# Opening of a hybrid gated-attention trunk: squares and scales of the second half's rows spread over the modulation's steps, products in three parts, one minimum pinned

## The chip, the cores and the metric

One NeuronCore of a Trainium2 chip runs the whole kernel. The metric is the device time of one execution in microseconds; the kernel before has a median of 1246.13 us over three runs (1244.64 to 1246.9).

## What is computed

One layer of a decoder trunk over 1024 rows of width 1024, all in float32. A conditioning vector gives shift and scale; the rows are normalised and modulated; one large projection of them feeds two gated linear attentions and their gates; both branches are merged and projected out. What matters here is the beginning:

```python
c_act = jax.nn.silu(c)
mod = c_act @ ada_w[l] + ada_b[l]
shift, scale, gate = jnp.split(mod, 3, axis=-1)
h = rms_norm(x, norm_w[l]) * (1.0 + scale[:, None, :]) + shift[:, None, :]
proj = h @ w_in[l]
...
log_a = jax.nn.log_sigmoid((ga @ alpha_w + alpha_b).astype(jnp.float32)) / GLA_GATE_TAU
```

The first columns of `proj` that are made are query and key of the second attention (GLA); the last line gives the decay of its four heads.

## The kernel before

**Arithmetic.** Each float32 operand of a large product is split into two parts of a faster type, `hi` by ScalarE's cast (L195) and `lo` by VectorE's subtraction (L196), and a product is the three matmuls hi*hi, hi*lo, lo*hi (`n` = 0, 1, 2 in `product`, L343).

**The opening** (L357 to L423) is written in the order in which TensorE, ScalarE and VectorE shall run it: those three are under a manual schedule from L158 to `order.close()` at L423. Behind that a scheduler orders the instructions. Each engine runs its own queue in order. The rows of `x` come in two halves of 512, each in four tiles of 128 rows. A half is normalised by `norm_x`: ScalarE squares a tile and sums (L204), takes a root (L206), VectorE inverts it (L207) and scales the tile in place (L208). `transpose_x` turns column block `d` of the four tiles on TensorE (L215) into one PSUM tile, which ScalarE copies out (L217). `make_h` applies the modulation on ScalarE (L224) and splits (L195, L196).

**The modulation** of the eight column blocks comes in five steps, `blocks` = (0), (1, 2), (3, 4), (5, 6), (7). For each step `load_mod` brings the weights, `add_mod` sums the upper half of the rows on VectorE (L256, L258), `mm_mod` does the lower half on TensorE (L268), `end_mod` adds both on VectorE (L274), sums over partitions on TensorE (L278) and leaves `modv` and `amul` (L281, L283), which `make_h` needs. While one step's column blocks go into the products, the next step is made: the loop at L368 interleaves `products(d, ns)`, which are six matmuls for each `n` (six groups of 128 columns: four for q, two for k, in the PSUM tiles `pd_177`, `pd_178` and `sc_ps`), with the steps of the next block. Step `bi == 3` also normalises the second half of the rows (L387).

**Behind the loop** stand two transposes and two `make_h` of the second half, the products of block 7, `make_ga` for the first half (L332, copied out by L334), and the six accumulators' copies `qk_out` on VectorE (L322, L324). `first_group` then does the products of the second half, and the generator `alpha_side` computes the decays of the four heads in pieces woven between them: two small products (L904), a bias (L906), a minimum on VectorE (L908) and a sum (L909), exponential (L914), logarithm (L917), a difference (L918) and an exponential (L921). Each `yield` says how many units of TensorE's work pass before the next piece.

**Loads** all go through SyncE's queue in the order written: weights of steps 0 and 1, three blocks of `w_in` between them, then step 2 and so on; the second half of `x` is asked for after step `bi == 1`. PSUM tiles `pm` come from a pool of two (`mtile`), so a third waits until the first has been read; the tiles `pd` also are two.

## Time and profile before

| what | value |
|---|---|
| median of 3 runs | 1246.13 us (1244.64 to 1246.9) |
| the profiled execution: its time, its span | 1243.66 us, 1242.0 us |
| TensorE busy | 1202.8 us (97%) |
| VectorE, ScalarE, GpSimd busy | 759.9, 535.3, 115.7 us |
| mean granted TensorE clock | 0.993 |
| moved by DMA | 168.82 MB |

The time of the profiled execution is 1.66 us over its span, which runs from the first instruction to the last. In the profile PE is TensorE, DVE VectorE, ACT ScalarE, POOL GpSimd and SP SyncE. A row of the instructions in order of time has start, duration (both us), engine, line, operation, the tile written and those read, and in brackets how long the engine was idle before it and whose end released it. A stage's row has for each engine the busy time and the count of instructions, then the granted TensorE clock, the share of time that the DMA engines were busy, and GB/s.

### The profile page before, as it was taken

The page shows a single profiled execution, that of the slowest core. Times are in us where ns is not written, and L with a number is a line of the kernel's source. Part 1 is how long each engine was busy: PE and PEld are TensorE (multiplying, and loading weights), DVE is VectorE, ACT ScalarE, POOL GpSimd, SP SyncE. Part 2 cuts the span into 40 slices and gives each one's busy share as a digit, 9 for nine tenths or more (in the row PEclk, how much of TensorE's full clock was granted, in tenths as well). Part 3 has the DMA queues.
Part 4 walks back from the last instruction along what each step waited for, and adds up shares of the span by engine and source line. Part 5 has one row for each costly group of instructions (what it writes and reads, how often), then busy time and mean ns, then how long its engine had stood idle before and what let it go on. Part 6 is the DMA issues. An engine that isn't in the chain of part 4 may idle for free.

```text
span 1242.0 us, 20840 instructions
## 1 busy us (share of the span) xinstructions
PE 1202.8 (97%) x8627; PEld 996.6 (80%) x8627; DVE 759.9 (61%) x1225; ACT 535.3 (43%) x786; POOL 115.7 (9%) x201
## 2 busy tenths in 40 slices
PE   5999999999999999999999999999999999998997
PEld 3676889889798888788887878877888887787786
DVE  5635535584848466877774366785422758979443
ACT  5547643434434234334323324457643644454222
POOL 4100000202111121011110101011100000000000
PEclk9989999999999999999999999999999999999999
DMA  9714010744544267265251112244547456235202
GB/s 325 258 52 136 24 28 19 260 157 145 170 151 147 81 200 244 96 187 166 74 186 52 51 35 69 75 156 169 184 158 243 154 186 195 77 102 178 110 35 101
DMA packets 126928, 168.82 MB, mean 136 GB/s; under 512 B 7019, under 2 KB 97185, under 8 KB 126834
## 3 DMA queue, kind: packets, MB, share of 16 engines
q1 hardware_dynamic: 115234, 129.53, 33.4%
q0 software_dynamic: 11552, 37.97, 8.0%
q8 instruction: 67, 1.10, 0.4%
q14 instruction: 27, 0.22, 0.1%
q10 hardware_dynamic: 48, 0.01, 0.0%
HBM read 125.53 MB, written 41.94 MB: 135 GB/s over the span
## 4 chain that ended last, share of the span: by engine, by line
PE 59%; issue 23%; DVE 8%; DMA 4%; ACT 3%; POOL 2%; SPq 0%; POOLq 0%; DVEq 0%; ACTq 0%
PE pd L518 14%; PE pd L1377 9%; PE sc_ps L1377 5%; PE pm L1377 4%; PE pd L343 3%; PE pd L620 2%; PE pd L621 2%; PE pd L622 2%; PE sc_ps L343 1%; DVE b L196 1%; PE pm L825 1%; PE pd L1147 1%; PE pd L1148 1%; PE pd L1149 1%; DMA b<-yh 1%
## 5 line engine op out<-in xcount | busy, mean ns | idle before, releaser
L518 PE MATMUL pd<-b,b 128*128 128x512 f32 x1632 | 386.7, 393 | 0.0
L518 PEld LDWEIGHTS pd<-b,b 128*128 128x128 f32 x1632 | 302.4, 188 | 64.3 <-issue 0.7
L1377 PE MATMUL pd<-b,b 128*128 128x512 f32 x720 | 175.5, 395 | 3.0 <-DVE b L930 1.5
L1377 PEld LDWEIGHTS pd<-b,b 128*128 128x128 f32 x720 | 134.4, 189 | 35.7 <-DVE b L930 1.9
L196 DVE TENSOR_TENSOR b<-b,b 128x1024 fp32r<-128x1024 f32 (+2 forms) x99 | 102.5, 1045 | 92.0 <-ACT b L195 75.3
L195 ACT CAST b<-b 128x1024 fp32r<-128x1024 f32 (+2 forms) x99 | 86.7, 888 | 109.1 <-PE pd L518 16.9
L1320 DVE TENSOR_TENSOR b<-b,b 128x1024 fp32r<-128x1024 f32 x56 | 68.2, 1222 | 68.8 <-ACT b L1319 50.5
L1319 ACT CAST b<-b 128x1024 fp32r<-128x1024 f32 x56 | 58.4, 1050 | 65.3 <-PE pd L1377 19.1
L1377 PE MATMUL sc_ps<-b,b 128*128 128x512 f32 x324 | 79.0, 391 | 0.9 <-ACT scT L770 0.9
L1377 PE MATMUL pm<-b,b 128*128 128x512 f32 x300 | 72.7, 390 | 3.3 <-DVE b L1320 3.3
L577 PE MATMUL pd<-b,b 128*128 128x256 f32 x256 | 74.6, 291 | 0.0
L579 PE MATMUL pd<-b,b 128*128 128x256 f32 x256 | 72.5, 283 | 0.0
L578 PE MATMUL pd<-b,b 128*128 128x256 f32 x256 | 72.4, 283 | 0.0
L1377 PEld LDWEIGHTS sc_ps<-b,b 128*128 128x128 f32 x324 | 60.4, 188 | 14.2 <-ACT scT L770 1.4
L1377 PEld LDWEIGHTS pm<-b,b 128*128 128x128 f32 x300 | 56.6, 189 | 15.6 <-DVE b L1320 3.7
L343 PE MATMUL pd<-b,b 128*128 128x512 f32 x192 | 56.6, 431 | 4.8 <-DVE b L322 2.6
L1298 DVE TENSOR_TENSOR b<-b,b 128x1024 fp32r<-128x1024 f32 x36 | 45.1, 1262 | 18.1 <-ACT b L1297 10.3
L1235 POOL DMA_DIRECT2D ws<-b x64 | 34.6, 541 | 192.6 <-DVE b L1229 87.3
L620 PE MATMUL pd<-b,b 128*128 128x512 f32 x128 | 51.3, 401 | 0.0
L343 PEld LDWEIGHTS pd<-b,b 128*128 128x128 f32 x192 | 37.3, 203 | 17.2 <-issue 3.4
L712 ACT COPY xb<-b 128x512 f32<-128x512 f32 x48 | 29.4, 620 | 48.8 <-PE sc_ps L692 26.6
L621 PE MATMUL pd<-b,b 128*128 128x512 f32 x128 | 50.0, 390 | 0.0
(269 smaller groups left out, 2010.6 us busy)
## 6 DMA issues: line engine op xcount, KB each, us to landing
b<-in_w_in_dram SPq DMA_DIRECT2D x66, 512.0 KB, 4.1
ws<-b POOLq DMA_DIRECT2D x64, 256.0 KB, 3.4
b<-ws SPq DMA_DIRECT2D x32, 512.0 KB, 4.4
b<-in_x_dram SPq DMA_DIRECT2D x16, 512.0 KB, 5.6
b<-in_ada_w_dram SPq DMA_DIRECT2D x32, 256.0 KB, 6.5
b<-in_w_branch_dram SPq DMA_DIRECT2D x16, 512.0 KB, 4.4
b<-h SPq DMA_DIRECT2D x14, 512.0 KB, 4.0
b<-in_w_in_dram SPq DMA_DIRECT2D x24, 256.0 KB, 3.8
```

The source lines that it names most:

```text
L195: nc.scalar.copy(hi, src)
L196: nc.vector.tensor_sub(lo, src, hi.bitcast(F32))
L343: nc.tensor.matmul(accs[f], wg(a, d, f), b[d][:, half * 512:half * 512 + 512], start=(d == 0 and n == 0), stop=(d == KT - 1 and n == 2))
L518: nc.tensor.matmul(ps[0:w, th * 512:(th + 1) * 512], a[:, k, 0:w], b[:, th * 512:(th + 1) * 512], start=(k == 0 and n == 0), stop=(k == KT ...
L577: nc.tensor.matmul(o, lh, hi[:, k % 4, :], start=(k == 0), stop=False)
L578: nc.tensor.matmul(o, lh, lo[:, k % 4, :], start=False, stop=False)
L579: nc.tensor.matmul(o, ll, hi[:, k % 4, :], start=False, stop=(k == KT - 1))
L620: nc.tensor.matmul(o, lh, hi[:, k % 2, :], start=(k == 0), stop=False)
L621: nc.tensor.matmul(o, lh, lo[:, k % 2, :], start=False, stop=False)
L1319: nc.scalar.copy(hi, t)
L1320: nc.vector.tensor_sub(lo, t, hi.bitcast(F32))
L1377: nc.tensor.matmul(o, a[:, sl], c, start=(p in (1, 5) and kt == 0 and n == 0), stop=(kt == 3 and n == 2), skip_group_check=True)
```

## The change

`norm_x` is cut into `square_x` (ScalarE's square and root) and `scale_x` (VectorE's inverse and scale), `transpose_x` into `turn_x` (TensorE) and `copy_x` (ScalarE); the computation is the same. In the opening the order changes: in the first step's loop `mm_mod(1)` and `end_mod(1)` stand between the three parts of the products, and block 3 is turned behind them, to be copied out within the next `make_h` loop. In step `bi == 3` two tiles of the second half are squared and scaled ahead of the products, the other two are squared behind the transposes and scaled behind `end_mod(4)`. Behind the loop, block 7's first products come ahead of the transposes, `make_h(1, 0)` behind all its products, and `make_h(1, 1)` behind the third `qk_out`. In `alpha_side` the minimum is kept in program order, and the pauses change.

```diff
--- before.py
+++ after.py
@@ -196,27 +196,35 @@
         nc.vector.tensor_sub(lo, src, hi.bitcast(F32))
         return hi, lo
 
-    def norm_x(half, xs):
-        for i, xt in enumerate(xs):
-            t = half * 4 + i
-            acc, r = ssx[:, t:t + 1], rsx[:, t:t + 1]
-            junk = S.get([D])
-            nc.scalar.activation(junk, xt, AF.Square, accum_out=acc)
-            S.free(junk)
-            nc.scalar.activation(r, acc, AF.Sqrt, bias=eps_t, scale=1.0 / D)
-            nc.vector.reciprocal(r, r)
-            nc.vector.tensor_scalar_mul(xt, xt, r)
-
-    def transpose_x(half, xs, d):
+    def square_x(t, xt):
+        acc, r = ssx[:, t:t + 1], rsx[:, t:t + 1]
+        junk = S.get([D])
+        nc.scalar.activation(junk, xt, AF.Square, accum_out=acc)
+        S.free(junk)
+        nc.scalar.activation(r, acc, AF.Sqrt, bias=eps_t, scale=1.0 / D)
+
+    def scale_x(t, xt):
+        r = rsx[:, t:t + 1]
+        nc.vector.reciprocal(r, r)
+        nc.vector.tensor_scalar_mul(xt, xt, r)
+
+    turned = {}
+
+    def turn_x(half, xs, d):
         if d % 2 == 0:
             hT[half, d // 2] = S.get([2, 512])
-        pt = mtile()
+        turned[half, d] = mtile()
         for i in range(4):
-            nc.tensor.transpose(pt[:, i * P:(i + 1) * P], xs[i][:, d * P:(d + 1) * P], ident)
-        dst = hT[half, d // 2][:, d % 2, :]
-        nc.scalar.copy(dst, pt)
+            nc.tensor.transpose(turned[half, d][:, i * P:(i + 1) * P], xs[i][:, d * P:(d + 1) * P], ident)
         if d == KT - 1:
             S.free(*xs)
+
+    def copy_x(half, d):
+        nc.scalar.copy(hT[half, d // 2][:, d % 2, :], turned.pop((half, d)))
+
+    def transpose_x(half, xs, d):
+        turn_x(half, xs, d)
+        copy_x(half, d)
 
     def make_h(half, d):
         b = hT[half, d // 2][:, d % 2, :]
@@ -356,7 +364,9 @@
     load_wg(3)
     load_wg(4)
     load_mod(2)
-    norm_x(0, x_t)
+    for i in range(4):
+        square_x(i, x_t[i])
+        scale_x(i, x_t[i])
     vec_rows(rows_a, 24, R_SH)
     transpose_x(0, x_t, 0)
     add_mod(0)
@@ -370,6 +380,8 @@
         nxt = range(blocks[bi + 1][0], sum(blocks[bi + 1])) if more else ()
         for d in ds:
             make_h(0, d)
+            if (0, d + 2) in turned:
+                copy_x(0, d + 2)
         if not more:
             break
         for d in nxt:
@@ -378,21 +390,30 @@
         if nd == 1:
             for d in nxt:
                 transpose_x(0, x_t, d)
+            products(d0, (0,))
+            mm_mod(bi + 1)
+            products(d0, (1,))
+            end_mod(bi + 1)
+            products(d0, (2,))
+            turn_x(0, x_t, nxt[-1] + 1)
+        else:
+            late = x_t2 if bi == 3 else ()
+            for i, xt in enumerate(late[:2]):
+                square_x(4 + i, xt)
+                scale_x(4 + i, xt)
             products(d0, (0, 1))
-            mm_mod(bi + 1)
-            products(d0, (2,))
-            end_mod(bi + 1)
-        else:
-            products(d0, (0, 1))
-            transpose_x(0, x_t, nxt[0])
-            if bi == 3:
-                norm_x(1, x_t2)
+            if bi > 1:
+                transpose_x(0, x_t, nxt[0])
+            for i, xt in enumerate(late[2:]):
+                square_x(6 + i, xt)
             mm_mod(bi + 1)
             products(d0, (2,))
             for d in nxt[1:]:
                 transpose_x(0, x_t, d)
             products(d0 + 1, (0,))
             end_mod(bi + 1)
+            for i, xt in enumerate(late[2:]):
+                scale_x(6 + i, xt)
             products(d0 + 1, (1, 2))
         if bi == 0:
             load_wg(5)
@@ -402,14 +423,13 @@
             load_mod(4)
         elif bi == 1:
             x_t2.extend(load_x(t) for t in range(4, 8))
+    products(KT - 1, (0,))
     for d in range(2):
         transpose_x(1, x_t2, d)
-    for d in range(2):
-        make_h(1, d)
-    products(KT - 1, (0,))
     for f in range(NG):
         for n in (1, 2):
             product(0, KT - 1, f, n)
+    make_h(1, 0)
     ga4, aw4 = S.get([T]), S.get([512])
     nc.gpsimd.memset(aw4, 0.0)
     for j in range(4):
@@ -420,6 +440,8 @@
     for f in range(NG):
         g_state[("q", f) if f < 4 else ("k", f - 4)] = qk_t[f]
         qk_out(f, 0, accs[f])
+        if f == 2:
+            make_h(1, 1)
     order.close()
 
     def first_group():
@@ -905,11 +927,11 @@
                                      start=True, stop=True)
                     nc.scalar.activation(zb[:, th * 512:(th + 1) * 512], pz, AF.Identity,
                                          bias=vec[:, R_AB + h:R_AB + h + 1])
-                nc.vector.tensor_scalar_min(m, zb, 0.0)
+                tc.keep_in_program_order(nc.vector.tensor_scalar_min(m, zb, 0.0))
                 nc.vector.scalar_tensor_tensor(zb, m, 2.0, zb, ALU.mult, ALU.subtract)
                 zs[h] = zb
                 alphas[h] = m
-                yield 4
+                yield 9 if h == 0 else 2
             for zb in zs.values():
                 nc.scalar.activation(zb, zb, AF.Exp)
             yield 4
@@ -920,7 +942,7 @@
             for h, zb in zs.items():
                 nc.scalar.activation(alphas[h], alphas[h], AF.Exp, scale=1.0 / TAU)
                 S.free(zb)
-            yield 6
+            yield 4
         S.free(ga4, aw4)
 
     def silu_done(store, key):
```

What this makes of the queues can't all be read from the diff. The rows below are the instructions of one engine in the order of its queue: line, operation, tile written and tiles read with their numbers, and shape. Lines of the change are those of its own file, about 8 higher at first and 22 higher later.

On **VectorE**, the end of step `bi == 3`: the sums of `add_mod(4)`, the second half's scales, the sum of `end_mod(4)` (`scT<-scT,pm`) and its `modv` and `amul`. Before:

```order
L258 SCALAR_TENSOR_TENSOR scT<-b_339,cs,scT 128x256 x3
L207 RECIPROCAL rsx<-rsx 128x1
L208 TENSOR_SCALAR b_425<-b_425,rsx 128x1024
L207 RECIPROCAL rsx<-rsx 128x1
L208 TENSOR_SCALAR b_427<-b_427,rsx 128x1024
L207 RECIPROCAL rsx<-rsx 128x1
L208 TENSOR_SCALAR b_429<-b_429,rsx 128x1024
L207 RECIPROCAL rsx<-rsx 128x1
L208 TENSOR_SCALAR b_431<-b_431,rsx 128x1024
L274 TENSOR_TENSOR scT<-scT,pm_565 128x256
L281 TENSOR_TENSOR modv<-pm_583,vec 128x2
L283 SCALAR_TENSOR_TENSOR amul<-modv,vec 128x1
```

In the change:

```order
L266 SCALAR_TENSOR_TENSOR scT<-b_344,cs,scT 128x256 x3
L208 RECIPROCAL rsx<-rsx 128x1
L209 TENSOR_SCALAR b_425<-b_425,rsx 128x1024
L208 RECIPROCAL rsx<-rsx 128x1
L209 TENSOR_SCALAR b_427<-b_427,rsx 128x1024
L282 TENSOR_TENSOR scT<-scT,pm_561 128x256
L289 TENSOR_TENSOR modv<-pm_579,vec 128x2
L291 SCALAR_TENSOR_TENSOR amul<-modv,vec 128x1
L208 RECIPROCAL rsx<-rsx 128x1
L209 TENSOR_SCALAR b_429<-b_429,rsx 128x1024
L208 RECIPROCAL rsx<-rsx 128x1
L209 TENSOR_SCALAR b_431<-b_431,rsx 128x1024
```

Two of the four pairs of reciprocal and scale now stand behind the step's end.

On **ScalarE**, the second half's first blocks: copies of the turned blocks (`b<-pm`), the modulation (ACTIVATE with `modv`), the casts, and the copy of `make_ga` (`b_640<-pm_651` before, `b_637<-pm_648` in the change). Before:

```order
L217 COPY b_603<-pm_604 128x512
L217 COPY b_603<-pm_610 128x512
L224 ACTIVATE b_603<-b_603,modv,amul 128x512
L195 CAST b_143<-b_603 128x512
L224 ACTIVATE b_603<-b_603,modv,amul 128x512
L195 CAST b_144<-b_603 128x512
L217 COPY b_779<-pm_780 128x512
L195 CAST b_822<-b_777 128x1024
L334 COPY b_640<-pm_651 128x512
L224 ACTIVATE b_779<-b_779,modv,amul 128x512
L195 CAST b_145<-b_779 128x512
```

In the change:

```order
L223 COPY b_609<-pm_610 128x512
L223 COPY b_609<-pm_616 128x512
L232 ACTIVATE b_609<-b_609,modv,amul 128x512
L195 CAST b_143<-b_609 128x512
L223 COPY b_779<-pm_780 128x512
L195 CAST b_822<-b_777 128x1024
L342 COPY b_637<-pm_648 128x512
L232 ACTIVATE b_609<-b_609,modv,amul 128x512
L232 ACTIVATE b_779<-b_779,modv,amul 128x512
L195 CAST b_144<-b_609 128x512
L195 CAST b_145<-b_779 128x512
```

The modulation of block 1 of the second half and its cast (`b_144`) stood ahead of the copy of `make_ga` and stand behind it, and block 2's modulation comes in between.

On **VectorE** again, the end of `first_group` and the first heads of `alpha_side`: `b_966` and `b_965` belong to head 0, `b_1000` and `b_999` (before), `b_1041` and `b_1040` (in the change) to head 1; `pd_177`, `pd_178` and `sc_ps` are the accumulators that `qk_out` empties; the rows that write `xb` begin the attention of head 0. Before:

```order
L908 TENSOR_SCALAR b_966<-b_965 128x1024
L909 SCALAR_TENSOR_TENSOR b_965<-b_966,b_965 128x1024
L196 TENSOR_TENSOR b_1075<-b_951,b_1074 128x1024
L196 TENSOR_TENSOR b_1139<-b_1043,b_1138 128x1024
L918 TENSOR_TENSOR b_966<-b_966,b_965 128x1024
L908 TENSOR_SCALAR b_1000<-b_999 128x1024
L322 TENSOR_SCALAR b_662<-pd_177 128x512
L909 SCALAR_TENSOR_TENSOR b_999<-b_1000,b_999 128x1024
L322 TENSOR_SCALAR b_663<-pd_177 128x512
L322 TENSOR_SCALAR b_664<-pd_178 128x512
L324 COPY b_666<-sc_ps 128x512
L653 TENSOR_TENSOR xb<-b_662,b_966 128x32x8
```

In the change:

```order
L930 TENSOR_SCALAR b_966<-b_965 128x1024
L931 SCALAR_TENSOR_TENSOR b_965<-b_966,b_965 128x1024
L196 TENSOR_TENSOR b_1071<-b_951,b_1070 128x1024
L196 TENSOR_TENSOR b_1139<-b_1031,b_1138 128x1024
L940 TENSOR_TENSOR b_966<-b_966,b_965 128x1024
L330 TENSOR_SCALAR b_659<-pd_177 128x512
L330 TENSOR_SCALAR b_661<-pd_178 128x512
L675 TENSOR_TENSOR xb<-b_659,b_966 128x32x8
L330 TENSOR_SCALAR b_660<-pd_177 128x512
L330 TENSOR_SCALAR b_662<-pd_178 128x512
L332 COPY b_663<-sc_ps 128x512
L196 TENSOR_TENSOR b_1135<-b_1029,b_1134 128x1024
```

The minimum of head 1 stood ahead of the first `qk_out`; now it comes six rows behind the last row shown. On TensorE, the two small products for head 1 stood ahead of the last products of the second half and stand behind them; from its 368th instruction on its order is the same as before, and so are SyncE's and GpSimd's whole orders.

## The prediction

> **What bounds the kernel now.** I read the page first, then the waits of TensorE, then TensorE's instructions in order of time.
>
> ```profile
> span 1242.0 us, 20840 instructions
> ...
> PE 1202.8 (97%) x8627; PEld 996.6 (80%) x8627; DVE 759.9 (61%) x1225; ACT 535.3 (43%) x786; POOL 115.7 (9%) x201
> ```
> ```profile
> PE pm L278 <- DVE scT L274: 4.7, 2, 4.0
> PE pd L343 <- DVE b L322: 2.6, 1, 2.6
> PE pd L343 <- ACT b L195: 2.2, 2, 2.0
> ```
> TensorE is busy 97% of the span, so time is won only where it stands idle or slow. The waits (total, times, longest) name three long ones on lines that the change touches. All three lie in the first 120 us:
>
> ```profile
> 23.01 1.07 PE L268 MATMUL pm<-b,cs 128*32 128x512 f32 x8
> 25.52 0.95 PE L278 MATMUL pm<-ones,scT 128*128 128x1 f32 x8
> 28.47 1.43 PE L343 MATMUL pd<-b,b 128*128 128x512 f32 x4 [2.01 <-ACT b L195]
> ...
> 37.76 0.95 PE L278 MATMUL pm<-ones,scT 128*128 128x1 f32 x8
> ...
> 58.90 0.61 PE L343 MATMUL sc_ps<-b,b 128*128 128x512 f32 x2
> 63.55 0.98 PE L278 MATMUL pm<-ones,scT 128*128 128x1 f32 x4 [4.04 <-DVE scT L274]
> ...
> 75.75 1.91 PE L332 MATMUL pm<-b,wga 128*16 128x512 f32 x16 [0.20 <-DVE pm L328]
> ...
> 111.32 1.88 PE L904 MATMUL pm<-b,b 128*128 128x512 f32 x4
> ...
> 118.78 0.96 PE L343 MATMUL pd<-b,b 128*128 128x512 f32 x3 [2.59 <-DVE b L322]
> ```
> **A** is the 2.01 us before 28.47: `end_mod(1)` is through, and the next products wait until `make_h(0, 1)` has used its result. **B** is the 4.04 us before 63.55: `end_mod(4)` waits for a VectorE sum. **C** is the 2.59 us before 118.78: a product waits for a `qk_out`. A and B have an aftermath, which the stages show (the column after POOL's is the granted clock):
>
> ```profile
> 29.30:32.60 3.30, 3.30 (x9) 2.61 (x8) 2.78 (x6) 2.14 (x5) 0.00 (x0) 0.50 1.05 384
> ...
> 64.40:69.80 5.40, 5.40 (x14) 4.13 (x15) 1.01 (x3) 1.43 (x2) 1.50 (x2) 0.50 0.25 100
> ```
> ```profile
> 20.11 0.85 PE sc_ps L343 x2
> ...
> 44.32 0.44 PE pm L215 x4
> ...
> 52.84 0.91 PE pd L343 x4
> ...
> 64.54 1.92 PE pd L343 x4
> ```
> After each the clock was 0.50 for a while; in the chain four products then take 1.92 us instead of 0.91. One product is 0.228 us warm, six are 1.37, twelve 2.73; four transposes are 0.44.
>
> [...]
>
> **Part A: products in three parts.** TensorE's work stays the same; `mm_mod(1)` moves ahead of six products, `end_mod(1)` ahead of six, and four transposes come in behind them. That puts 1.37 + 0.44 = 1.81 us between `end_mod(1)` and the products of tile 1, where 2.01 us were idle. But two other things can now end last:
>
> ```profile
> 15.18 1.38 SPq L242 DMA_DIRECT2D b<-in_ada_w_dram  x2
> ```
> ```profile
> b<-in_ada_w_dram SPq DMA_DIRECT2D x1, 256.0 KB, 6.0
> ```
> ```profile
> 21.01 2.33 DVE L258 SCALAR_TENSOR_TENSOR scT<-b,cs,scT 128x512 f32<-128x512 f32 x3
> 24.17 0.69 DVE L274 TENSOR_TENSOR scT<-scT,pm 128x512 f32<-128x512 f32 x1 [0.83 <-PE pm L268]
> 28.45 0.69 DVE L196 TENSOR_TENSOR b<-b,b 128x512 fp32r<-128x512 f32 x1 [1.59 <-ACT b L195]
> 29.82 2.57 DVE L196 TENSOR_TENSOR b<-b,b 128x512 fp32r<-128x512 f32 x5 [0.68 <-ACT b L195]
> 35.25 0.69 DVE L274 TENSOR_TENSOR scT<-scT,pm 128x512 f32<-128x512 f32 x1
> ```
> ```profile
> 27.80 0.62 ACT L195 CAST b<-b 128x512 fp32r<-128x512 f32 x1
> 28.32 0.82 ACT L224 ACTIVATE b<-b,modv,amul 128x512 f32<-128x512 f32 x1
> 33.55 0.58 ACT L217 COPY b<-pm 128x512 f32<-128x512 f32 x1 [2.11 <-PE pm L215]
> ```
> First the load. The last of the eight transfers of `load_mod(1)` is issued at 16.2 (the second of the pair from 15.18) and lands 6.0 us later, at 22.2. Before, `mm_mod(1)` began at 23.0 and never saw it; now TensorE is there when the first six products are through, at 20.96 (20.11 + 0.85), and waits for it, so its end comes at 23.2, not 24.1. Six products follow to 24.6. VectorE's share of the sum is done at 23.3 and its L274 at 24.1, in time. `end_mod(1)` (0.95) ends at 25.5, 1.0 us earlier than before; the 2.0 us through VectorE and ScalarE to the first product stay, so tile 1 starts at 27.5 instead of 28.47. TensorE idles 0.2 us there, and the cold stretch goes.
>
> Then VectorE. The subtraction of `make_h(0, 1)` comes 1.0 us earlier, but ScalarE now copies the turned tile 3 (0.58) before `make_h(0, 2)`, so the second group of subtractions moves from 29.82 to 29.4 only, and the sum for `end_mod(2)` from 35.25 to 34.8, done at 35.5. TensorE, warm, needs from 27.5: twelve products 2.73, `mm_mod(2)` 1.0, six products, four transposes, six products, 6.9 us in all: it is there at 34.4 and waits 1.2 us. `end_mod(2)` begins at 35.6 instead of 37.76. **A is worth 2.1 us**, though 3.8 were to be had (2.01 and some 1.75 of slow clock). If the clock stays low until about 25.8, since TensorE waited for the load, it is 0.9; if VectorE isn't late, 3.8.
>
> **Part B: squares and scales spread.** Eight VectorE steps (four reciprocals, four scales), paced by ScalarE's squares, stood ahead of the sum for `end_mod(4)`. Four stay ahead, and their squares start earlier.
>
> ```profile
> 53.19 0.92 ACT L195 CAST b<-xb 128x512 fp32r<-128x512 f32 x2
> ...
> 56.52 1.06 ACT L204 ACTIVATE b<-b 128x1024 f32<-128x1024 f32 x1
> ```
> ```profile
> 55.24 1.52 DVE L258 SCALAR_TENSOR_TENSOR scT<-b,cs,scT 128x256 f32<-128x256 f32 x3
> 58.03 0.16 DVE L207 RECIPROCAL rsx<-rsx 128x1 f32<-128x1 f32 x1 [1.26 <-ACT rsx L206]
> ...
> 62.32 0.75 DVE L208 TENSOR_SCALAR b<-b,rsx 128x1024 f32<-128x1024 f32 x1
> ```
> On the clock of before: the first square starts at 54.1, behind the casts, instead of 56.52; its root is there 1.5 us later (58.03 against 56.52), the second 1.4 after that, at 57.0 (a tile takes 1.4: from the first reciprocal, 58.03, to the fourth, 0.2 before 62.32, are three steps). VectorE is free of the modulation's sums at 56.8, makes two reciprocals and scales (0.16 and 0.75 each), and reaches the sum at 58.7, done at 59.1. TensorE finishes its products at 59.5: no stall, 0.4 us to spare. The two late squares run on ScalarE until 60.4, just when the modulation of tile 7 is due; the two late scales end at 62.2, and the transposes that need them now stand behind six more products, at about 64. So the 4.04 us go, and with them the cold clock: twelve products (1.92 for four, 0.85 for two, twice: 5.5 less 2.73) and a slow `end_mod` (0.98 for four steps where eight took 0.95), together about 3.2.
>
> Given back: `make_h(1, 1)` now stands behind the copy of `make_ga`. After those products TensorE has 1.37 + 0.88 of work (six products, eight transposes) while ScalarE does a copy, two ACTIVATEs and a cast, 0.58 + 0.82 + 0.82 + 0.62; that is 0.6 short, and the subtraction of 0.69 behind it costs another 0.5. The wait of 0.20 before 75.75 I take to stay. **B is worth 4.0 + 3.2 - 1.1 = 6.1.** The ends: 4.0 if VectorE is 2.1 us late for the sum and the clock holds, 7.2 if nothing is given back.
>
> **Part C: the pinned minimum.**
>
> ```profile
> 113.91 1.23 DVE L918 TENSOR_TENSOR b<-b,b 128x1024 f32<-128x1024 f32 x1 [2.19 <-ACT b L917]
> 117.43 0.69 DVE L908 TENSOR_SCALAR b<-b 128x1024 f32<-128x1024 f32 x1 [2.29 <-ACT b L906]
> 118.04 0.68 DVE L322 TENSOR_SCALAR b<-pd 128x512 f32<-128x512 f32 x1
> ```
> The minimum of head 1 stood on VectorE ahead of the first `qk_out` and waited 2.29 us for ScalarE. In the new order that `qk_out` comes right behind L918, at 115.1, done at 115.8 instead of 118.7. TensorE, which now has two products of `alpha_side` (the 1.88 us from 111.32) behind this place and not ahead of it, is there at 114.3 instead of 116.2, and waits 1.5 us. **C is worth 1.1 us** (0 if it only moves the wait, 2.6 if it vanishes).
>
> The stage behind runs at TensorE's pace in an order that from the 368th TensorE row on is as before, so what is won is kept. **Sum: 2.1 + 6.1 + 1.1 = 9.3.** The profiled execution took 1243.66 us (its span of 1242.0 and 1.66 around it), so 1234.4 for its like. The median of the three runs, 1246.13, lies 2.5 above it; taken from that, the forecast is **1236.8**.
>
> **Rivals.** (1) *The opening stays bound by its loads and by VectorE.* The transfer that lands at 22.2 and the sum at 34.8 speak for it; A gives 0.9, B 4.0, C nothing: 1241.2. Against it is B's working, which has little to do with loads. Chance 0.17. (2) *The gain is lost later*: a wait that is hidden now comes forward by as much, and the time is within 0.2% (2.5 us, about what a measurement of this kernel can tell from no change), say 1245. Few waits of TensorE behind 130 us speak for it. Chance 0.07. [...] Chance 0.05. (4) *Slower: head-of-line blocking on VectorE behind the pinned minimum.* The minimum of head 1 and its chain through ScalarE now stand ahead of the product that frees the first projection's accumulator:
>
> ```profile
> 136.34 1.22 DVE L930 TENSOR_TENSOR b<-b,pd 128x1024 f32<-128x1024 f32 x1 [1.11 <-ACT b L929]
> ```
> ```profile
> 146.27 0.68 PE L577 MATMUL pd<-b,b 128*128 128x256 f32 x1
> ```
> That product ends at 137.6, and TensorE takes the accumulator up at 146.27: 8.7 us to spare. From there each microsecond of delay costs one. I work its end out to about 138, so it decides from 8.7 us of delay on, and eats up the gain from 9.3 + 8.7 = 18.0 on. With 21, as if the chains of heads 2 and 3 came ahead as well, 12.3 are lost against 9.3 won: 1249.1. Chance 0.05.
>
> The forecast itself has 0.66. The range goes from all three stalls gone with nothing given back, 3.8 + 7.2 + 2.6 = 13.6, so 1232.5, to rival 1, 1241.2. Faster by over 0.2%: 0.66 + 0.17 + 0.05 = 0.88; within: 0.07; slower: 0.05.
>
> **What the new profile would show.** Right: no idle of 2 us before the products of tile 1 and the clock at 1.00 behind them; a short wait of `mm_mod(1)` for its load; about 1.2 us before `end_mod(2)`, for VectorE; none before `end_mod(4)`; about 1 us in the first products of the second half; about 1.5 us where C was. Wrong: a clock of 0.50 after 26 us, a long wait before `end_mod(4)`, or a new wait for the first accumulator near 137 us.

## The result

| | before | after |
|---|---|---|
| median | 1245.78 us (1242.98 to 1249.43, 6 runs) | 1236.90 us (1234.35 to 1239.09, 6 runs) |
| the profiled execution: time, span | 1243.66, 1242.0 us | 1236.45, 1234.7 us |
| mean granted TensorE clock | 0.993 | 0.997 |

The ratio of after to before is 0.9941 with a 95% interval of 0.9923 to 0.9959: faster by 0.6%. The forecast was 1236.8. One execution of the kernel with the 9 alone (below), which took 1839.93 us at a mean granted clock of 0.609, is left out of all figures.

### The profile page after: what moved, and what is told of

It reads as the page before. It is cut to its first block, busy times and chain, and to the rows that moved or that the text cites. A ratio compares the mean times of both kernels' runs of the same rounds, so it can differ in the third digit from the quotient of the medians.

```text
span 1234.7 us, 20836 instructions
## 1 busy us (share of the span) xinstructions
PE 1199.6 (97%) x8627; PEld 992.4 (80%) x8627; DVE 759.7 (62%) x1225; ACT 533.0 (43%) x785; POOL 116.4 (9%) x201
## 4 chain that ended last, share of the span: by engine, by line
PE 54%; issue 24%; DVE 7%; DMA 3%; ACT 3%; POOL 2%; POOLq 0%; SPq 0%; DVEq 0%; ACTq 0%
PE pd L540 14%; PE pd L1399 8%; PE sc_ps L1399 5%; PE pm L1399 3%; PE pd L642 2%; PE pd L643 2%; PE pd L644 2%; DVE b L196 1%; PE pd L351 1%; PE pm L847 1%; PE pd L1169 1%; PE pd L1170 1%; PE pd L1171 1%; DMA b<-yh 1%; PE pm L828 1%
## 5 line engine op out<-in xcount | busy, mean ns | idle before, releaser
L540 PE MATMUL pd<-b,b 128*128 128x512 f32 x1632 | 387.5, 394 | 0.0
L540 PEld LDWEIGHTS pd<-b,b 128*128 128x128 f32 x1632 | 302.4, 188 | 64.9 <-issue 1.4
L1399 PE MATMUL pd<-b,b 128*128 128x512 f32 x720 | 175.5, 395 | 3.5 <-DVE b L952 1.5
L1399 PEld LDWEIGHTS pd<-b,b 128*128 128x128 f32 x720 | 134.5, 189 | 36.4 <-ACT b L1341 2.0
L351 PE MATMUL pd<-b,b 128*128 128x512 f32 x192 | 53.3, 410 | 1.6 <-ACT b L195 0.9
L642 PE MATMUL pd<-b,b 128*128 128x512 f32 x128 | 51.3, 401 | 0.0
L643 PE MATMUL pd<-b,b 128*128 128x512 f32 x128 | 50.0, 390 | 0.0
L644 PE MATMUL pd<-b,b 128*128 128x512 f32 x128 | 49.9, 390 | 0.0
```

What stands on the lines that cost most here:

```text
L351: nc.tensor.matmul(accs[f], wg(a, d, f), b[d][:, half * 512:half * 512 + 512], start=(d == 0 and n == 0), stop=(d == KT - 1 and n == 2))
L540: nc.tensor.matmul(ps[0:w, th * 512:(th + 1) * 512], a[:, k, 0:w], b[:, th * 512:(th + 1) * 512], start=(k == 0 and n == 0), stop=(k == KT ...
L642: nc.tensor.matmul(o, lh, hi[:, k % 2, :], start=(k == 0), stop=False)
L643: nc.tensor.matmul(o, lh, lo[:, k % 2, :], start=False, stop=False)
L644: nc.tensor.matmul(o, ll, hi[:, k % 2, :], start=False, stop=(k == KT - 1))
L1399: nc.tensor.matmul(o, a[:, sl], c, start=(p in (1, 5) and kt == 0 and n == 0), stop=(kt == 3 and n == 2), skip_group_check=True)
```

## The profile after

The page's head and its busy times:

```profile
span 1234.7 us, 20836 instructions
...
PE 1199.6 (97%) x8627; PEld 992.4 (80%) x8627; DVE 759.7 (62%) x1225; ACT 533.0 (43%) x785; POOL 116.4 (9%) x201
```

TensorE does the same 8627 matmuls in 3.2 us less of busy time: the slow clock that is gone, less some 1.5 by which `mm_mod(1)` is stretched (below). The rest of the 7.3 is idle time. TensorE's instructions in order of time; the first row is the first product of the opening, the rows behind it answer to those of before (L276, L286, L340, L351, L540 were L268, L278, L332, L343, L518):

```profile
18.90 2.08 PE L351 MATMUL pd<-b,b 128*128 128x512 f32 x4 [0.20 <-ACT b L195]
21.76 2.52 PE L276 MATMUL pm<-b,cs 128*32 128x512 f32 x8
25.72 0.95 PE L286 MATMUL pm<-ones,scT 128*128 128x1 f32 x8
28.68 1.20 PE L351 MATMUL pd<-b,b 128*128 128x512 f32 x4
36.89 1.02 PE L286 MATMUL pm<-ones,scT 128*128 128x1 f32 x8 [0.79 <-DVE scT L282]
58.53 0.50 PE L286 MATMUL pm<-ones,scT 128*128 128x1 f32 x4
67.53 1.91 PE L340 MATMUL pm<-b,wga 128*16 128x512 f32 x16 [0.20 <-DVE pm L336]
72.61 0.49 PE L351 MATMUL pd<-b,b 128*128 128x512 f32 x1 [0.68 <-ACT b L195]
73.33 2.35 PE L351 MATMUL pd<-b,b 128*128 128x512 f32 x9 [0.23 <-DVE b L196]
95.19 1.91 PE L340 MATMUL pm<-b,wga 128*16 128x512 f32 x16
108.06 1.66 PE L351 MATMUL pd<-b,b 128*128 128x512 f32 x6 [0.45 <-DVE b L330]
```

The reader is to see no bracket where A stood (28.68) and where B stood (58.53), and 0.45 where C was 2.59. The stages, in the columns of the rows of before (the number behind POOL's is the granted clock), stand at full clock behind A's place and behind B's:

```profile
28.68:38.60 9.92, 9.13 (x48) 6.51 (x49) 6.91 (x13) 4.37 (x9) 0.18 (x1) 1.00 1.07 373
58.50:64.00 5.50, 5.50 (x32) 4.69 (x31) 2.87 (x7) 2.42 (x6) 2.15 (x3) 1.00 0.42 147
```

VectorE's rows show what was spread: the sum for `end_mod(4)` (L282 at 57.57) now stands behind two scales instead of four. And they show the first accumulator's product, L952, ending at 128.1:

```profile
30.62 2.57 DVE L196 TENSOR_TENSOR b<-b,b 128x512 fp32r<-128x512 f32 x5 [1.27 <-ACT b L195]
...
56.90 0.75 DVE L209 TENSOR_SCALAR b<-b,rsx 128x1024 f32<-128x1024 f32 x1
57.57 0.41 DVE L282 TENSOR_TENSOR scT<-scT,pm 128x256 f32<-128x256 f32 x1
...
106.18 1.23 DVE L940 TENSOR_TENSOR b<-b,b 128x1024 f32<-128x1024 f32 x1 [1.44 <-ACT b L939]
...
126.91 1.22 DVE L952 TENSOR_TENSOR b<-b,pd 128x1024 f32<-128x1024 f32 x1 [2.23 <-ACT b L951]
```

**Where the time came from.** The same TensorE instruction's start, before less after, grows along the program like this (rows of L343/L351, L278/L286, L332/L340; the last two from the two traces at the same TensorE instruction):

| place | before | after | gained so far | by this part |
|---|---|---|---|---|
| first product | 18.03 | 18.90 | -0.87 | the start, not the change |
| `end_mod(2)` | 37.76 | 36.89 | 0.87 | A: 1.74 |
| first `make_ga` | 75.75 | 67.53 | 8.22 | |
| second `make_ga` | 101.99 | 95.19 | 6.80 | B: 5.93, net of what was given back |
| 325 us of before | 325.13 | 315.94 | 9.19 | C: 2.39 |
| end of the span | 1242.0 | 1234.7 | 7.3 | lost behind 325: 1.9 |

The later start is a load of `x` that landed later in this execution (the slowest of the four took 6.4 us from issue to landing and not 5.4, and ScalarE waited 0.9 us for it); the other versions start between 18.14 and 19.49.

## The experiments

The comparisons below are to the kernel before on the same chip, whose median was 1245.34 us beside the kernels with A, B or C undone and the one with the second `make_h` early, 1244.86 beside B filled, the 9 alone and the two with the loads in time, and 1244.28 beside A filled and the 9 and the 2.

### A undone

```diff
-            products(d0, (0,))
+            products(d0, (0, 1))
             mm_mod(bi + 1)
-            products(d0, (1,))
-            end_mod(bi + 1)
             products(d0, (2,))
-            turn_x(0, x_t, nxt[-1] + 1)
+            end_mod(bi + 1)
```

(and block 3 is turned in the next step, as before.)

> The change with part A alone undone: the first step's products again in two parts, block 3 turned again in step 1. Theory (idle time cools the clock, and both are what A wins): about 2.0 us idle before the products of tile 1, a granted clock of 0.50 for about 3.4 us behind it, and the end of step 1 (the sums over partitions of end_mod(2)) 19.7 us after the first product, as before, and not 18.0 as in the change; total 1.7 us over the change, about 1238.6. Rival (the slow clock is not the gap's doing, or the load that TensorE now waits for gives A's gain back): the same idle of 2.0, but the clock stays at 1.00 behind it or that distance is 18.0 to 18.4; total within 0.4 us of the change.

Measured: 1238.31 us (1234.63 to 1240.46), ratio 0.9937 (0.9918 to 0.9957). TensorE in order of time, then the stage behind the stall:

```profile
19.06 2.08 PE L351 MATMUL pd<-b,b 128*128 128x512 f32 x4 [0.20 <-ACT b L195]
...
28.75 2.07 PE L351 MATMUL pd<-b,b 128*128 128x512 f32 x4 [2.01 <-ACT b L195]
39.23 0.95 PE L286 MATMUL pm<-ones,scT 128*128 128x1 f32 x8
```
```profile
28.75:34.00 5.25, 5.25 (x12) 4.02 (x13) 4.50 (x9) 2.94 (x6) 0.18 (x1) 0.50 1.06 387
```

The stall is back to the hundredth, and with it the clock of 0.50, in this run for at least the 5.25 us of the row, before for 3.42 us (29.25 to 32.67 us). From the first product to `end_mod(2)` pass 20.17 us, against 17.99 in the change and 19.73 before: A is worth 2.2 by this pair and 1.7 by the other. The total of 1.4 over the change can't be told from nothing: the two ratios overlap almost wholly.

### A's idle time filled

Is it the idle 2 us that cost, or the clock? The kernel without A again, with 8 products into a spare tile behind `end_mod(1)`, which is work that the reference doesn't ask for:

```diff
-            end_mod(bi + 1)
+            end_mod(bi + 1); fill = mtile(); [nc.tensor.matmul(fill, wg(0, 0, j % 4), h_hi[0][:, 0:512], start=True, stop=True) for j in range(8)]
```

> The kernel with A undone (2.01 us of idle, then 6.83 us at a clock of 0.50, 1238.3), with 8 products more, 8 x 0.228 = 1.8 us, into a spare tile, just where TensorE stands idle; the wait for ScalarE stays as long. It tells A's idle time from A's clock. Theory (all that A costs is the slow clock): the clock is 1.00 behind it, end_mod(2) comes about 17.3 us behind the first product and not 20.17, VectorE then being the late one, and the whole 2.0 to 2.8 us under 1238.3, so 1235.5 to 1236.3, no worse than the change. [...]

Measured: 1237.96 us (1236.22 to 1239.06), ratio 0.9952 (0.9939 to 0.9964).

```profile
19.49 2.07 PE L351 MATMUL pd<-b,b 128*128 128x512 f32 x4 [0.20 <-ACT b L195]
...
27.12 2.10 PE L396 MATMUL pm<-b,b 128*128 128x512 f32 x8
29.27 1.21 PE L351 MATMUL pd<-b,b 128*128 128x512 f32 x4
...
37.02 0.95 PE L286 MATMUL pm<-ones,scT 128*128 128x1 f32 x8
```
```profile
29.27:34.50 5.23, 5.23 (x28) 3.50 (x29) 4.48 (x9) 3.53 (x7) 0.18 (x1) 1.00 1.05 385
```

Tile 1 starts 9.78 us behind the first product, as in the change (28.68 - 18.90), so the filled kernel reaches it no sooner. But the clock stands at 1.00 behind it, and `end_mod(2)` comes 17.53 us behind the first product, not 20.17. So, with the loads where they are, all that A cost was the slow clock. This pair of kernels, the same but for 8 products in a gap of 2.01 us, has the clock at 0.50 behind the gap (28.75 to 34.00 us) and at 1.00 behind the products that fill it (29.27 to 34.50 us).

The total missed its expectation by 1.7 us and lies nearer to the 1238.3 of the kernel with A undone: by the totals the fill won nothing that can be told from noise, and the reading above rests on the trace. The trace also shows where the time went: at 325 us of before this kernel is 9.12 us ahead of before, as far as the change (9.19), and at 500 only 7.34. Between the two, VectorE waited for a store:

```profile
377.62 1.23 DVE L196 TENSOR_TENSOR b<-b,b 128x1024 fp32r<-128x1024 f32 x1 [2.60 <-DMA ws<-b]
```

A subtraction whose tile is still being written out to DRAM stands at the head of VectorE's queue, the totals of a head stand behind it, and TensorE waits 1.59 us for those. In the executions profiled of before and of the change VectorE has no such wait. Others have it at the same place: 0.99 us with A undone (0.1 lost there), 3.07 us in the kernel with the 9 and the 2 below (2.0 lost). What makes the store late in one profiled execution and not in the other was not settled; as a wait that a total may or may not hold, it blurs differences of 2 us.

### The spread of squares and scales undone

```diff
-            for i, xt in enumerate(late[:2]):
-                square_x(4 + i, xt)
-                scale_x(4 + i, xt)
...
-            for i, xt in enumerate(late[2:]):
-                square_x(6 + i, xt)
+            for i, xt in enumerate(late):
+                square_x(4 + i, xt)
+                scale_x(4 + i, xt)
...
-            for i, xt in enumerate(late[2:]):
-                scale_x(6 + i, xt)
```

> The change with the spread of squares and scales alone undone: all four tiles of the second half squared and scaled at one place again, behind the turn of block 7; the products of block 7 stay ahead of the transposes. Theory (VectorE's four scales ahead of the sum make the stall): an idle time of 3.5 to 4.2 us before the sums over partitions of end_mod(4), a granted clock of 0.50 for 3.4 to 6.8 us behind it, total 5.5 to 7 us over the change, about 1243. Rival (half of B's gain comes from the products of block 7 put ahead of the transposes, which can run while VectorE scales): under 3 us over the change.

Measured: 1244.28 us (1240.86 to 1246.89), ratio 0.9985 (0.9972 to 0.9998), which doesn't touch the change's interval. TensorE's rows, then VectorE's last scale and the sum:

```profile
62.42 0.90 PE L286 MATMUL pm<-ones,scT 128*128 128x1 f32 x4 [4.04 <-DVE scT L282]
74.70 1.91 PE L340 MATMUL pm<-b,wga 128*16 128x512 f32 x16 [0.22 <-DVE pm L336]
```
```profile
61.19 0.75 DVE L209 TENSOR_SCALAR b<-b,rsx 128x1024 f32<-128x1024 f32 x1
61.86 0.41 DVE L282 TENSOR_TENSOR scT<-scT,pm 128x256 f32<-128x256 f32 x1
```

The stall of 4.04 us is B, to the hundredth, and the clock was 0.51 on average over the 6.08 us behind it (62.42 to 68.50 us). The first `make_ga` comes 7.2 us later than in the change. The whole is 7.4 longer by the medians, and 0.44% (5.5 us) by the two ratios. B is the change's largest part by far, and this is the one part that the totals alone show.

### B's idle time filled

The kernel without the spread, with 17 products more ahead of `end_mod(4)`'s, into the tile that it overwrites:

```diff
-        pm = mtile()
+        pm = mtile(); [nc.tensor.matmul(pm, wg(0, 6, j % 4), h_hi[6][:, 0:512], start=True, stop=True) for j in range(17 if bi == 4 else 0)]
```

> The kernel without the spread squares and scales (stall B back, 4.04 us), with 17 products more, 17 x 0.228 = 3.9 us, written to the tile that end_mod(4) overwrites, just where TensorE stands idle; the wait for VectorE stays as long. It tells the two halves of B apart. Theory (of B's 7.2 us 4.0 are the wait and 3.2 the slow clock that the idle brings): some 0.2 us of idle, the clock 1.00 behind it, the second half's first make_ga about 3.2 us earlier than without the 17, and 1244.3 - 3.2 = 1241.1 in all. Rival (the slow stretch comes at that place for another reason, or the products behind are late for other engines anyway): as without the 17, 1244.3.

Measured: 1239.95 us (1239.37 to 1245.32), ratio 0.9966 (0.9953 to 0.9979).

```profile
58.96 4.01 PE L283 MATMUL pm<-b,b 128*128 128x512 f32 x17
63.09 0.61 PE L286 MATMUL pm<-ones,scT 128*128 128x1 f32 x4
...
72.23 1.91 PE L340 MATMUL pm<-b,wga 128*16 128x512 f32 x16 [0.20 <-DVE pm L336]
```
```profile
63.09:69.20 6.11, 6.11 (x33) 5.21 (x34) 1.01 (x3) 2.21 (x4) 1.50 (x2) 1.00 0.21 86
```

TensorE waits as long, only busy, and the clock stays at 1.00. From `end_mod(4)` to `make_ga` pass 9.14 us instead of 12.28: the slow clock behind B costs 3.14, and the prediction had 3.2. The whole is 4.3 us shorter than without the useless products by the medians, and 0.19% (2.4 us) by the ratios, whose intervals overlap a little; the 3.14 of the trace is the firm number.

### C's three edits undone

```diff
-                tc.keep_in_program_order(nc.vector.tensor_scalar_min(m, zb, 0.0))
+                nc.vector.tensor_scalar_min(m, zb, 0.0)
...
-                yield 9 if h == 0 else 2
+                yield 4
...
                 S.free(zb)
-            yield 4
+            yield 6
```

> The change with the edits in the decay's generator alone undone (minimum not pinned, pauses of 4, 4, 4, 6). Theory (the minimum of head 1 ahead of the first copy of an accumulator makes the stall): the minimum again ahead of that copy on VectorE, an idle time of about 2.6 us on TensorE there against 0.45 in the change, total 2.1 us over the change, about 1239.0. Rival (half of C's gain comes from a weight load that lands earlier relative to its cast, since buffers were dealt otherwise): the load's wait of 0.3 us stays as in the change and TensorE idles only about 1.7 us, total 1.2 over the change.

Measured: 1239.10 us (1237.02 to 1241.89), ratio 0.9948 (0.993 to 0.9966). VectorE, then TensorE:

```profile
106.85 1.23 DVE L940 TENSOR_TENSOR b<-b,b 128x1024 f32<-128x1024 f32 x1 [2.12 <-ACT b L939]
110.37 0.70 DVE L930 TENSOR_SCALAR b<-b 128x1024 f32<-128x1024 f32 x1 [2.30 <-ACT b L928]
110.98 0.68 DVE L330 TENSOR_SCALAR b<-pd 128x512 f32<-128x512 f32 x1
```
```profile
111.72 0.96 PE L351 MATMUL pd<-b,b 128*128 128x512 f32 x3 [2.37 <-DVE b L330]
```

The mechanism stands as the prediction had it: head 1's minimum waits for ScalarE at the head of the queue, and the `qk_out` that TensorE needs stands behind it. Up to the second `make_ga` this trace runs level with the change's (6.81 gained against 6.80); at 325 us of before it has 5.73 against 9.19, so the three edits are worth 3.5 here and 2.4 by the two original traces. The difference goes with the clock: here it was 0.60 on average behind the stall (111.80 to 115.90 us), while behind the 2.59 us of before it stayed at 1.00 (119.00 to 122.00 us). The sign of the rival (part of the gain is a weight load that lands earlier) didn't come: the idle is 2.37 us and not 1.7. But a load has its share: with the edits undone ScalarE's cast waits 0.94 us for its load again, against 0.26 in the change, so the earlier load goes with the edits (more on it below).

**Which of the three edits?** Not the pin. With the pin and without it the order of every engine is the same, row for row, with the change's pauses and with those of before; so it can change no time, and it wasn't run. The pauses do it all.

### Of the pauses, the 9 alone

```diff
-                tc.keep_in_program_order(nc.vector.tensor_scalar_min(m, zb, 0.0))
+                nc.vector.tensor_scalar_min(m, zb, 0.0)
...
-                yield 9 if h == 0 else 2
+                yield 9 if h == 0 else 4
...
-            yield 4
+            yield 6
```

> Of the three edits in alpha_side only the first pause of 9 is kept; the pin is gone and the other pauses are 4 and 6 as before. Up to the first head's chain the order of TensorE, VectorE and ScalarE is then that of the change. Theory (C goes because head 1's two small products and its minimum come later, which the pause of 9 alone does): less than 0.6 us of idle where C was, the clock 1.00 behind it, 1236.9 give or take 1. Rival (the other pauses are needed): a time of 1239, that without the three edits, through a new wait where heads 2 and 3 come.

Measured: 1247.57 us (1242.14 to 1250.17), ratio 1.0017 (1.0004 to 1.003): slower than before by a little, and the theory's time missed by nearly 11 us. The rival's new waits came, but its 1239 was missed by far too. C itself is gone, as the theory had it. TensorE's row where C was, and from its waits (total, times, longest) the ones that neither before nor the change has at such length:

```profile
107.41 1.66 PE L351 MATMUL pd<-b,b 128*128 128x512 f32 x6 [0.62 <-DVE b L330]
```
```profile
PE pm L828 <- ACT b L807: 5.0, 2, 3.1
PE sc_ps L714 <- DVE tot L717: 4.7, 2, 2.9
```

Both are lines of the attention that follows `alpha_side`. Its first row on TensorE (L682) comes at 172.4 us in this kernel and at 166.4 in the change; its last head is 13.6 us late (822.2 against 808.6). The mean clock was 0.99 from 330 to 500 us, from 500 to 700 and from 700 to 865, and 1.00 in the change's stretches that answer to these (318 to 492, 492 to 692, 692 to 852). Not all of it need be the pauses' doing: ahead of the longest wait on L714, VectorE waited 3.13 us for a store here too (`yg<-b`, at 381.8 us), and how much of the 11 us that took isn't shown. The pauses add up to 49 units of TensorE's work here, to 39 in the change and to 44 before.

### The 9 and the 2, the last pause as before

```diff
                 S.free(zb)
-            yield 4
+            yield 6
```

> The change with only the last pause put back from 4 to 6 (and the pin as in the change). The pauses of alpha_side add up to 44 units in the kernel before, 39 in the change, 49 with the 9 alone, which took 1247.7, and 43 here. Theory (what the 9 alone lost, some 11 us behind 146 us, is that alpha_side ends 5 units later than before, so that the attention of head 0 begins later and TensorE waits for its totals): with 43 units it ends as early as before, no wait of 2 us or more between 150 and 800 us, 1236.9 give or take 1.5. Rival (the order behind is so finely set that any other spacing brings such waits): two or more waits over 1.5 us there, 1240 or more.

Measured: 1236.83 us (1235.94 to 1238.07), ratio 0.9943 (0.993 to 0.9957), as fast as the change. The attention's first row comes at 165.5. TensorE's longest wait on its lines:

```profile
PE sc_ps L714 <- DVE tot L717: 2.0, 2, 1.8
```

That wait is the late store again (3.07 us on VectorE), not the pauses. So the 2 is as much a part of the change as the 9: the 9 takes head 1 out of `qk_out`'s way, and with the shorter pauses behind it the attention of head 0 is back at its place. That the sum of the pauses (43 here) is what matters is the reading that fits both runs; no run varies it alone.

### The second `make_h` early

```diff
-    make_h(1, 0)
+    for d in range(2):
+        make_h(1, d)
...
-        if f == 2:
-            make_h(1, 1)
```

> The change with the second half's block 1 modulated again directly behind block 0, ahead of the clearing of the PSUM tile for the gate projection. Theory (VectorE's queue decides: the clearing then stands behind a second subtraction that waits for ScalarE): the 0.68 and 0.23 us idle before the second block's products go, but the gate projection waits about 1.3 us more for its cleared tile; total 0.2 to 0.6 us over the change, about 1237.3. Rival (the modulation behind the copy is a plain loss): no new wait, total 0.9 us under the change, about 1236.0.

Measured: 1236.05 us (1235.51 to 1238.26), ratio 0.9926 (0.9909 to 0.9942).

```profile
69.02 1.91 PE L340 MATMUL pm<-b,wga 128*16 128x512 f32 x16 [1.57 <-DVE pm L336]
95.24 1.91 PE L340 MATMUL pm<-b,wga 128*16 128x512 f32 x16
```

The 0.68 and 0.23 us in the first products of the second half are gone, and 1.57 us stand ahead of `make_ga` instead of 0.20: VectorE clears that tile behind the second subtraction, for which it waits in order. The second `make_ga` comes 76.20 us behind the first product, in the change 76.29. So the wait that the theory named came (1.57 us, 1.3 expected), and the total came where the rival had it, 0.85 under the change; the two intervals overlap, so the totals don't decide. By the trace the give-back in B was a choice between two waits of about the same size.

### Loads and splits in time

`load_mod(1)` is asked for ahead of `load_wg(2)`, and in steps 0 and 1 the second block's weight split stands behind `end_mod`:

```diff
-    load_wg(2)
     load_mod(1)
+    load_wg(2)
...
-        for d in nxt:
+        for d in nxt[:1] if bi < 2 else nxt:
             prep_wg(d)
...
             end_mod(bi + 1)
+            prep_wg(nxt[1])
             products(d0, (2,))
```

(the copy of block 3 also stands behind both `make_h`; step 1 has the same move.)

> The change with load_mod(1) asked for ahead of the third block of w_in, and with the second block's weight split of steps 0 and 1 behind end_mod, so that neither the load nor VectorE is late for the modulation. Theory (what is left of A is the load of step 1, some 1.5 us inside mm_mod(1), and VectorE's 0.79 us ahead of end_mod(2)): mm_mod(1) takes about 1.0 us and not 2.52, no idle before end_mod(2), the whole 1.5 to 2.3 us under the change, 1234.6 to 1235.4. Rival (the opening is bound by its loads as a whole; the next load or the next split is then the late one): no gain, 1236.9, with a new wait of 1 to 2 us in the next 20 us.

Measured: 1234.85 us (1232.99 to 1236.84), ratio 0.9917 (0.99 to 0.9933). TensorE:

```profile
18.57 2.08 PE L351 MATMUL pd<-b,b 128*128 128x512 f32 x4 [0.20 <-ACT b L195]
...
21.20 1.71 PE L276 MATMUL pm<-b,cs 128*32 128x512 f32 x8
...
35.14 0.95 PE L286 MATMUL pm<-ones,scT 128*128 128x1 f32 x8
...
93.42 1.91 PE L340 MATMUL pm<-b,wga 128*16 128x512 f32 x16
```

`mm_mod(1)` takes 1.71 us and not 2.52, so the load is still a little late (1.0 was expected); the idle before `end_mod(2)` is gone, and the second `make_ga` comes 74.85 us behind the first product, 1.44 sooner than in the change. Tile 1 starts 8.75 us behind the first product (27.32 - 18.57), 1.03 sooner than in the change: with the load sooner, half of A's idle time can be had as well. The opening is not bound by its loads as a whole.

### The same, with ScalarE's half of `make_h(1, 1)` early

```diff
     make_h(1, 0)
+    b = hT[1, 0][:, 1, :]
+    nc.scalar.activation(b, b, AF.Identity, bias=modv[:, 0, 1:2], scale=amul[:, 1:2])
+    nc.scalar.copy(h_hi[1][:, 512:1024], b)
...
-            make_h(1, 1)
+            nc.vector.tensor_sub(h_lo[1][:, 512:1024], b, h_hi[1][:, 512:1024].bitcast(F32))
```

> The kernel of the run before this one, and ScalarE's part of make_h(1, 1) directly behind make_h(1, 0), with VectorE's part left behind the third qk_out. Theory (the 0.68 and 0.23 us in the first products of the second half are ScalarE's and VectorE's lateness, and with the subtraction left where it is the clearing of the next tile isn't delayed): none of these three waits is left, another 0.9 us, 1233.7 to 1234.5. Rival (as in the run where the whole make_h came early, the wait turns up before the first product of make_ga): about 1 us idle before make_ga, the time that of the run before.

Measured: 1234.38 us (1232.88 to 1235.99), ratio 0.9913 (0.9895 to 0.9931).

```profile
19.37 2.08 PE L351 MATMUL pd<-b,b 128*128 128x512 f32 x4 [0.20 <-ACT b L195]
...
66.47 1.91 PE L340 MATMUL pm<-b,wga 128*16 128x512 f32 x16 [0.20 <-DVE pm L336]
...
92.74 1.91 PE L340 MATMUL pm<-b,wga 128*16 128x512 f32 x16
```

None of the three waits is left, and `make_ga` has its 0.20 again: the second one comes 73.37 us behind the first product, 2.9 sooner than in the change. This is the fastest version here; its interval overlaps the change's, so that the step from the one to the other is shown by the trace of the opening, not by the totals.

## Why the prediction was right

The forecast's case came, with the signs that it named: full clock behind A, a longer `mm_mod(1)`, a short wait before `end_mod(2)` for VectorE, none before `end_mod(4)`, 0.91 us (0.68 + 0.23) in the second half's first products where about 1 was given, and a rest where C was.

- **A, 2.1 predicted, 1.7 and 2.2 measured.** The load made `mm_mod(1)` end 5.4 us behind the first product (24.28 - 18.90), where 5.2 were worked out, so tile 1 starts 0.3 later against the first product than predicted; VectorE waits 1.27 us for ScalarE's copy, and TensorE waits 0.79 for VectorE, not 1.2. The working counted 2.01 us of idle and 1.75 of clock. Of the idle time nothing was won, since tile 1 starts no sooner than with A undone (9.78 us behind the first product against 9.69); what the part won is the clock. The kernel with the loads in time, where tile 1 comes at 8.75, shows that it was the load of `mm_mod(1)` that took the idle time's worth.
- **B, 6.1 predicted, 5.9 measured.** The wait is 4.04 and the clock 3.14, 7.2 as predicted; up to the first `make_ga` the table has 7.35 (8.22 - 0.87). The give-back was a little under-sized: 0.91 by the two waits that the rows show, but 1.42 by the table (8.22 - 6.80), as the products around the waits are also further apart, where 1.1 was given. The sum for `end_mod(4)` was done with 0.55 us to spare (57.57 + 0.41 to 58.53), 0.4 having been predicted.
- **C, 1.1 predicted, 2.4 measured, the mis-sized term.** The step that failed is the stall left over: 1.5 us were worked out, 0.45 came. The prediction took the first `qk_out` to come behind L918 at the time that the row had, 113.91. But that row came behind a cast of ScalarE that waited for a load, 1.18 us before and 0.26 after, and it comes 0.93 us sooner against the second `make_ga`: 11.92 us behind it before (113.91 - 101.99), 10.99 after (106.18 - 95.19).

```profile
109.40 1.05 ACT L195 CAST b<-b 128x1024 fp32r<-128x1024 f32 x1 [1.18 <-DMA b<-in_w_in_dram]
```
```profile
101.67 1.06 ACT L195 CAST b<-b 128x1024 fp32r<-128x1024 f32 x1 [0.26 <-DMA b<-in_w_in_dram]
```

  This is the edits' own work too, not chance. SyncE issues the pair of loads ahead of that cast sooner: the first 1.16 us ahead of the second `make_ga` (95.19) and not 1.11 behind it (101.99). The rows of before and of after:

```profile
103.10 1.29 SPq L554 DMA_DIRECT2D b<-in_w_in_dram  x2
```
```profile
94.03 2.60 SPq L576 DMA_DIRECT2D b<-in_w_in_dram  x2
```

  It is so in all ten kernels with the pause of 9 (1.14 to 1.17 us ahead, the cast's wait 0.20 to 0.36) and in neither of the two without it (1.11 behind, the wait 0.94 and 1.18). In those two the first issue waits for products of the second `make_ga`; in the others the profile shows no such wait. SyncE's order is the same in before and after, so it must be the buffer that the load writes, or when that came free; which is not shown. The prediction also credited the pin, which does nothing, with the pauses' work.
- **What hid it.** The parts add up to 10.1 instead of 9.3, the start was 0.87 late, and 1.9 were lost behind 325 us; the medians differ by 8.9. About 1.6 us lie in four short waits of TensorE that are longer in the profiled execution of after than in that of before: at 835 us (1.20 against 0.93), 857 (0.77 against 0.49), 1038 (0.95 against 0.63) and 1146 (0.90 against 0.20). The other versions that are as fast lose between 0.4 (A undone) and 3.8 (loads and splits in time) there, with no order to it, so I take it for the spread of executions; that is not shown. That the median came within 0.1 us of the forecast is luck: parts that were off, a late start and a later loss happened to cancel.

The rivals: (1) is out, since B is whole and A more than the clock's share of 0.9. (2) came in part, as the 1.9, and not to the size it named. That the slow clock behind A was not A's doing is ruled out by the two kernels that differ only in a filled gap (0.50 behind the idle 2.01 us, 1.00 behind the fill). (4) did not come: the product that frees the accumulator, L952, ends at 128.1 us, and TensorE takes the accumulator up at 137.8, so there are 9.7 us to spare instead of 8.7. But its mechanism, one waiting instruction at the head of VectorE's queue with TensorE's need behind it, is C's own and the late store's: it is real here, at other places.

## What to carry over

Price a stall of TensorE as its idle time and the clock behind it, and find out by filling the gap with useless products which of the two it is: the fill costs one line and took 3.14 us out of B. Measure a part against the work just ahead of it (from the first product to a fixed instruction), since parts of 1 to 2 us drown in the spread of the totals. When a pause in a woven side job grows, look at what the job's end releases: here the longer pause paid only with shorter ones behind it.

## What the runs showed of the hardware

Whether the clock was slow behind a gap isn't read from the gap's length alone. Gaps with a slow clock behind them: 4.04 us before (0.50 from 63.39 to 70.21 us) and with the spread undone (0.51 on average from 62.42 to 68.50 us), 2.01 us before (0.50 from 29.25 to 32.67 us) and with A undone (0.50 from 28.75 to 34.00 us), 2.37 us with C undone (0.60 on average from 111.80 to 115.90 us), 3.31 us in the change (0.50 from 1129.22 to 1132.63 us). Gaps without: 2.59 us before (1.00 from 119.00 to 122.00 us) and 2.95 us in the kernel with the 9 alone (from 390.74 to 394.83 us, behind the gap, its products start 0.23 us apart, as at full clock). With the gap filled the clock was 1.00 both times (29.27 to 34.50 us with A's filled, 63.09 to 69.20 us with B's).

What sorts these cases is not shown: two runs fill a gap, and none varies the length or the place of one alone. Nor was the clock the same in every execution of a kernel: with A undone two of the six ran at the mean clock of the change's profiled execution, 0.997 (1234.63 and 1234.90 us), the other four at 0.991 to 0.995 (1237.38 to 1240.46 us).
